# Side tasks of the first feed forward layer with fp32 products in place of split ones

## The chip, the cores and the metric

The kernel runs on one core of one Trainium2 chip. The metric is the device time of one execution in microseconds: three runs of the kernel before gave 1909.66, 1913.12 and 1913.76 us, median 1913.12 us. The profiled execution was a fourth one.

## The reference

Two blocks run one after the other on a sequence of 256 positions of width 1024, all in fp32. The first block has two layers; each is a mixer (three kinds of attention) and a feed forward layer. The second block also has two layers: the first mixes by long convolutions (Hyena), the second by attention; both have a cross attention on a memory and sixteen experts. Cut to what the change touches:

```python
# first block, layer l
x = x + hybrid_mixer(rms_norm(x, norm_mix[l]), ...)
x = x + jnp.square(jax.nn.relu(rms_norm(x, norm_mlp[l]) @ w_up[l])) @ w_down[l]     # 1024 -> 4096 -> 1024

# second block: needs nothing of x
h = jnp.sin(fr * (feats @ w1 + b1))                       # 256 x 33 -> 256 x 64
h = jnp.sin(fr * (h @ w2 + b2))                           # 256 x 64
h = (h @ w3).reshape(L, 2, 2, 768) * decay                # the filter layer: order, direction, channel
h = h / (jnp.sum(jnp.abs(h), axis=(0, 2), keepdims=True) + 1e-6)
k_fft = jnp.fft.rfft(two_sided(h), axis=0)                # the spectra
mem_n = rms_norm_2(mem, mem_norm_g)
mk, mv = jnp.split(mem_n @ w_mem_kv[i], 2, axis=-1)       # the memory projections, i = 0, 1; 256 + 256 columns
```

## The kernel before, in words

A product of two fp32 matrices is mostly done as three fp32r products (`mm3`, L302): each operand is split into a rounded part (hi, xh) and a rest (lo, xl), and hi·hi, lo·hi and hi·lo are summed in PSUM. The rounding is a copy on ScalarE (L290); the rest is a subtraction (L291) that GpSimd and VectorE take in turn. A product written with plain fp32 operands needs no split; the trace shows it as two TensorE instructions.

The first feed forward layer (`mlp`, about 246 to 540 us of the trace) is a sequence of units. A unit has a `prep` (load and split a weight tile) and a `run` (its products); `Pipe` prepares two units ahead of the one that it runs. Weight tiles of 1 MB come through a ring of five buffers over the queue of SyncE, in program order: a load waits until its buffer is free. A buffer becomes free with the last instruction that reads it. Up products go to `psT`, down products to `acc`.

What the second block needs of constants and memory is computed beside this layer, in a generator (`mlp0_tasks`). After each unit `Pipe.tick` lets it take one step, up to its next `yield`, and so the instructions of a step stand, on every engine's in-order queue, between those of two units. `filters_task` first loads small tables and makes the two sine layers (`sin_layer`, on VectorE and ScalarE), with `h2` as their result on 128 partitions: the 64 hidden rows stand there twice. Then it goes through four blocks (order o, half n of the channels). A block has two steps of the filter layer (`psf`, L1119 and L1120, one for each 128 positions, two directions d in each), their sums and differences over the directions (`hx`, then split into `hs`), the column sums of the absolute values (`sab`, `psn`, `nrm`), and two steps of spectra (L303 to L305 into `psf`, then `ke` and `kx`). `memory_task` normalises and transposes the memory (`Norm`, two halves of 512 columns) and computes, for both layers, keys (`psT`) and values (`psM`). `Norm` transposes on TensorE into PSUM (L343); ScalarE copies the rounded part out (L346), and VectorE the rest (L347). A PSUM buffer is free once both have read it. Four PSUM buffers (`A`) serve `psT`, `psf`, `psn`, `psM` and the transposes of the memory in turn.

The order on each engine is fixed when the program is built. Before the last down products the layer waits for the side tasks to end (`pipe.join(side)`), and all later stages follow it.

Of the kernel before, what the change touches and what calls it, by code (L numbers as in the profile page):

```python
# [22 lines left out]
T = 256  # L23
# [176 lines left out]
def build(ctx, tc, I, C, out, upto="all", dbg=None):  # L200
# [124 lines left out]
    class Norm:  # L325
# [3 lines left out]
        def __init__(self, src, g, pool=None, psum=None, split=True):  # L329
            self.src, self.g, self.ps = src, g, psum or B  # L330
            if split:
                self.xh = (pool or xtp).tile([128, 8, T], F32R, tag="xh", name="xh")
                self.xl = (pool or xtp).tile([128, 8, T], F32R, tag="xl", name="xl")
            self.ss = small.tile([128, 2, 2], F32, tag="ss", name="ss")
            self.halves = 0
            self.r = self.R = None

        def half(self, n):
            for k2 in (4 * n, 4 * n + 2):
# [690 lines left out]
    def stream(units, pool):  # L1030

        ahead = deque()
        for u in units + [None, None]:
            if u:
                hl.append(pool)
                u.prep()
                hl.pop()
                ahead.append(u)
            if len(ahead) == 3 or not u:
                ahead.popleft().run()  # L1040
            yield

# [17 lines left out]
    def filters_task(ring, kd):  # L1060

        with tc.tile_pool(name="fl", bufs=1) as fp:
# [26 lines left out]
            hst = fp.tile([128, T], F32R, name="fhst")  # L1089
# [3 lines left out]
            S.activation(hst, h2, AF.Copy)  # L1093
            V.tensor_tensor(hst[64:], h2[64:], hst[64:].bitcast(F32), op=ALU.subtract)
# [5 lines left out]
            for o in range(2):  # L1100
                for n in range(2):
                    c = slice(384 * n, 384 * n + 384)
                    w3 = fp.tile([128, 2, 384], F32, name="fw3")
                    for d in range(2):
                        nc.sync.dma_start(w3[64 * d:64 * d + 64], I["hy_filt_w3_2"][0].rearrange("k (o d c) -> k o d c", o=2, d=2)[:, o, :, c])
                    w3h = fp.tile([128, 2, 384], F32R, name="fw3h")
                    w3l = fp.tile([64, 2, 384], F32R, name="fw3l")
                    S.activation(w3h, w3, AF.Copy)
                    G.tensor_tensor(w3l, w3[:64], w3h[:64].bitcast(F32), op=ALU.subtract)
                    hs = {op: [fp.tile([128, 2, 384], F32R, tag=f"h{op}{i}", name="hs") for i in range(2)] for op in (ALU.add, ALU.subtract)}  # L1110
                    sab = fp.tile([128, 384], F32, tag="sab", name="sab")
                    yield
                    for t in range(2):
                        hd = []
                        for d in range(2):
# [26 lines left out]
                    for part, op in ((0, ALU.add), (1, ALU.subtract)):  # L1142
# [3 lines left out]
                        for t in range(2):  # L1146
                            mm3(pp[t], Fh[:, t, part], Fl[:, t, part], hs[op][0][:, t], hs[op][1][:, t], True, True)
# [10 lines left out]
    def memory_task(ring, mp, sp, m, kvd):  # L1158

        nm = Norm(m, gain("mem_norm_g_2"), mp, A)  # L1160
        yield from nm.task(lambda n: True)
        for l in range(2):
# [3 lines left out]

            def put_k(j, ps):
                V.tensor_tensor(kv[:, 0], ps, nm.R[:, None, :].to_broadcast([128, 2, T]), op=ALU.mult)

            def put_v(ps):  # L1170
                for t in range(2):
                    evac(kv[:, 1, t], ps[t][:, :256], t, nm.r[:, t:t + 1])
# [658 lines left out]
    def mlp0_tasks(ring):  # L1831
        yield from filters_task(ring, kd)
        with tc.tile_pool(name="memp", bufs=1) as mp, tc.tile_pool(name="mems", bufs=3) as sp:
# [4 lines left out]
            yield from memory_task(ring, mp, sp, m, kvd)  # L1838
# [183 lines left out]
```

## Time and profile before

| | us |
|---|---|
| three runs: lowest, median, highest | 1909.66, 1913.12, 1913.76 |
| the profiled execution's own time | 1915.09 |
| its span, first to last instruction | 1913.3 |
| TensorE busy | 1643.7 (86%) |
| VectorE busy | 981.1 (51%) |
| ScalarE busy | 665.7 (35%) |
| GpSimd busy | 540.2 (28%) |
| mean granted TensorE clock | 0.952 |

Busy time is an average over stages with different limits: in the page's 40 slices of 47.8 us TensorE is busy nine tenths through most of the first half, and from slice 24 on the DMA engines are. In a row of the trace PE is a product on TensorE and PEld its weight load; DVE is VectorE, ACT ScalarE, POOL GpSimd, SPq the queue of SyncE. A form such as `64*128 64x384` means weights on 64 rows and 128 columns, and 384 columns streamed. A product's duration includes the time until its end has come out, so consecutive products overlap; the pace is read from their starts. A bracket at a row's end holds the idle time of the engine before it, and whose result ended it.

### The profile page before, as it was taken

The numbers are of one execution on the slowest core, as the hardware profiler recorded it, in microseconds if no ns is written. First come the engines' busy times: TensorE is split into PE (matmuls) and PEld (weight loads), VectorE is DVE, ScalarE is ACT, GpSimd is POOL, SyncE is SP. The second block draws the span as 40 slices with busy tenths as digits, with TensorE's granted clock in tenths as the row PEclk, the third lists the DMA queues.
The fourth block names the chain that finished last, engine by engine and source line by source line (L and its number), as shares of the span: only waits on it lengthen the run. The fifth ranks groups of instructions, "written<-read, shape, count | busy, mean of one in ns | idle before, by whom it ended". The sixth has DMA issues, their size and how long they took to land. (4 is left out here: it accounts for less than half of the span.)

```text
span 1913.3 us, 27291 instructions
## 1 busy us (share of the span) xinstructions
PE 1643.7 (86%) x11139; PEld 1201.3 (63%) x11139; DVE 981.1 (51%) x1642; ACT 665.7 (35%) x1100; POOL 540.2 (28%) x330
## 2 busy tenths in 40 slices
PE   8899988999998999999989989676667999766665
PEld 7898977788988979899978765222224655211221
DVE  7987467666489865754568763010104873100102
ACT  4346444454443464545444432000003552000000
POOL 4532455754445325444434220000002220000001
PEclk9999999999999999999999989898988999898987
DMA  6443554455633435755443679999999768999997
GB/s 237 128 133 123 179 181 157 162 194 170 211 125 102 161 124 174 259 196 182 152 160 121 221 285 420 425 425 425 425 413 335 265 247 362 425 426 424 426 420 254
DMA packets 136516, 490.42 MB, mean 256 GB/s; under 512 B 11152, under 2 KB 32067, under 8 KB 115911
## 3 DMA queue, kind: packets, MB, share of 16 engines
q1 hardware_dynamic: 135919, 488.11, 67.8%
q8 instruction: 87, 1.43, 0.3%
q10 hardware_dynamic: 472, 0.57, 0.1%
q14 instruction: 38, 0.31, 0.0%
HBM read 483.41 MB, written 5.24 MB: 255 GB/s over the span
## 5 line engine op out<-in xcount | busy, mean ns | idle before, releaser
L291 POOL TENSOR_TENSOR lo<-w,hi 128x1024 fp32r<-128x1024 f32 (+3 forms) x163 | 379.1, 2327 | 806.5 <-ACT hi L290 776.4
L290 ACT ACTIVATE hi<-w 128x1024 fp32r<-128x1024 f32 (+3 forms) x330 | 327.3, 997 | 347.7 <-PE psT L305 178.9
L304 PE MATMUL psT<-xh,lo 128*128 128x256 f32 x1328 | 382.1, 288 | 12.4 <-POOL lo L291 12.4
L303 PE MATMUL psT<-xh,hi 128*128 128x256 f32 x1328 | 388.6, 293 | 2.0 <-ACT hi L290 2.0
L305 PE MATMUL psT<-xl,hi 128*128 128x256 f32 x1328 | 381.6, 287 | 0.0
L291 DVE TENSOR_TENSOR lo<-w,hi 128x1024 fp32r<-128x1024 f32 (+3 forms) x167 | 223.2, 1337 | 145.4 <-ACT hi L290 144.7
L304 PEld LDWEIGHTS psT<-xh,lo 128*128 128x128 f32 x1328 | 259.5, 195 | 18.1 <-POOL lo L291 14.2
L303 PEld LDWEIGHTS psT<-xh,hi 128*128 128x128 f32 x1328 | 259.2, 195 | 10.1 <-issue 5.9
L305 PEld LDWEIGHTS psT<-xl,hi 128*128 128x128 f32 x1328 | 259.3, 195 | 1.8 <-issue 1.8
L1738 PE MATMUL psx<-w,late 128*32 128x256 f32 (+1 forms) x1024 | 155.3, 539 | 75.8 <-DMA w<-in_exp_w_up 40.5
L1738 PEld LDWEIGHTS psx<-w,late 128*32 128x32 f32 x1024 | 47.0, 115 | 181.5 <-issue 74.2
L1738 PE MATMUL psx<-w,xg 128*32 128x256 f32 (+1 forms) x1024 | 124.1, 538 | 36.6 <-DMA w<-in_exp_w_up 19.9
L1790 PE MATMUL psy<-w,late 128*32 128x512 f32 x576 | 95.3, 596 | 38.2 <-DMA w<-in_exp_w_down 34.3
L1774 ACT ACTIVATE yy<-psy,rslot 128x512 fp32r<-128x512 f32 (+1 forms) x17 | 11.3, 662 | 320.7 <-PE psy L1790 249.7
L1738 PEld LDWEIGHTS psx<-w,xg 128*32 128x32 f32 x1024 | 39.9, 116 | 117.5 <-issue 60.6
L305 PE MATMUL acc<-lo,hh 128*128 128x512 f32 x256 | 100.7, 393 | 1.9 <-POOL lo L291 1.9
L304 PE MATMUL acc<-hi,hlo 128*128 128x512 f32 x256 | 100.8, 394 | 0.0
L303 PE MATMUL acc<-hi,hh 128*128 128x512 f32 x256 | 100.5, 393 | 0.0
L1982 POOL TENSOR_TENSOR o<-X,gf 128x256 f32<-128x256 f32 (+1 forms) x6 | 6.1, 1042 | 326.5 <-DVE X L1780 326.5
L1775 DVE SCALAR_TENSOR_TENSOR yy<-psy,rslot,yy 128x512 fp32r<-128x512 f32 (+1 forms) x17 | 12.2, 719 | 163.4 <-ACT yy L1774 162.9
L1754 DVE TENSOR_TENSOR late<-late,psx 128x512 f32<-128x512 f32 (+1 forms) x16 | 8.1, 550 | 166.8 <-PE psx L1738 166.8
L1790 PEld LDWEIGHTS psy<-w,late 128*32 128x32 f32 x576 | 26.6, 109 | 102.6 <-DMA w<-in_exp_w_down 52.4
(494 smaller groups left out, 2945.3 us busy)
## 6 DMA issues: line engine op xcount, KB each, us to landing
w<-in_exp_w_gate SPq DMA_DIRECT2D x64, 1536.0 KB, 27.8
w<-in_exp_w_up SPq DMA_DIRECT2D x64, 1536.0 KB, 29.5
w<-in_exp_w_down SPq DMA_DIRECT2D x48, 1536.0 KB, 28.5
w<-in_w_in SPq DMA_DIRECT2D x39, 1024.0 KB, 5.1
w<-in_w_up SPq DMA_DIRECT2D x32, 1024.0 KB, 5.7
w<-in_w_down SPq DMA_DIRECT2D x32, 1024.0 KB, 6.8
w<-in_exp_w_down SPq DMA_DIRECT2D x18, 1024.0 KB, 14.3
w<-in_w_out SPq DMA_DIRECT2D x10, 1024.0 KB, 5.6
```

What stands on the lines that cost most here:

```text
L290: S.activation(hi, src, AF.Copy)
L291: next(lo_engines[0]).tensor_tensor(lo, src, hi.bitcast(F32), op=ALU.subtract)
L303: PE.matmul(ps, lh, rh, start=start, stop=False)
L304: PE.matmul(ps, ll, rh, start=False, stop=False)
L305: PE.matmul(ps, lh, rl, start=False, stop=stop)
L1738: mm = PE.matmul(pg[nm][n][32 * e:32 * e + 32, :c1 - c0], xg[gr // 2][:, k, 128 * (gr % 2) + 32 * e:128 * (gr % 2) + 32 * e + 32], wt[e][: ...
L1754: V.tensor_tensor(hid[:, c], sg[:, :n], pg["up"][i][:, :n], op=ALU.mult)
L1774: S.activation(yh, py, AF.Copy, scale=rs[:, 2, gr:gr + 1])
L1775: V.scalar_tensor_tensor(yl, py, rs[:, 2, gr:gr + 1], yh.bitcast(F32), op0=ALU.mult, op1=ALU.subtract)
L1790: PE.matmul(py[n][32 * e:32 * e + 32], hT[:, k, 32 * e:32 * e + 32], wt[e][:, k - k0, 512 * n:512 * n + 512], start=k == 0, stop=k == 5, t ...
L1982: G.tensor_tensor(o[:, t, c], X[:, t, c], gf[:, c], op=ALU.mult)
```

## The change

Three places of the side tasks lose their splits:

- Filter layer: the sum over 64 hidden rows was one product over 128 rows (both parts of `h2` against the rounded weights) and one over 64 rows (against the weights' rest), for each direction. Now each direction is one fp32 product over 64 rows; direction 0 uses partitions 0 to 63 and direction 1 partitions 64 to 127 (`tile_position`), and each has its own PSUM buffer. The weights `w3` come in half the size, in two buffers. The conversions of `h2` (`hst`) and `w3` (`w3h`, `w3l`) go.
- Spectra: the constant transform `F` and the sums `hs` stay fp32, and three fp32r products become one fp32 product. `F` is loaded alone; before, it took a ring buffer and was split into `Fh` and `Fl`.
- Memory projections: `Norm` gets a third form (`split=None`) that writes one fp32 tile by ScalarE alone. Keys and values are fp32 products straight from the ring's weight tiles, in 8 steps per layer where there were 11. `stream` goes.

```diff
         def __init__(self, src, g, pool=None, psum=None, split=True):
-            if split:
+            self.x = None
+            if split is None:
+                self.x = pool.tile([128, 8, T], F32, name="xT")
+            elif split:
...
                 for j in range(2):
                     k = k2 + j
+                    if self.x is not None:
+                        S.activation(self.x[:, k], ps[:, j], AF.Copy, scale=self.g[:, k:k + 1])
+                        continue
...
-            raw = ring.one(C["fwd"]).rearrange("p t (s f) -> p t s f", s=2)[:, :, :, :128]
-            Fh = fp.tile([128, 2, 2, 128], F32R, name="fFh")
-            Fl = fp.tile([128, 2, 2, 128], F32R, name="fFl")
-            S.activation(Fh, raw, AF.Copy)
-            V.tensor_tensor(Fl, raw, Fh.bitcast(F32), op=ALU.subtract)
+            F = fp.tile([128, 2, 2, 128], F32, name="fF")
+            nc.sync.dma_start(F, C["fwd"].rearrange("p t (s f) -> p t s f", s=2)[:, :, :, :128])
...
-            S.activation(hst, h2, AF.Copy)
-            V.tensor_tensor(hst[64:], h2[64:], hst[64:].bitcast(F32), op=ALU.subtract)
...
-                    w3 = fp.tile([128, 2, 384], F32, name="fw3")
+                    w3 = fp.tile([128, 384], F32, name="fw3", bufs=2)
...
-                    S.activation(w3h, w3, AF.Copy)
-                    G.tensor_tensor(w3l, w3[:64], w3h[:64].bitcast(F32), op=ALU.subtract)
...
+                        pd = [A("psf", [128, 384]) for _ in range(2)]
+                        for d in range(2):
+                            r = slice(64 * d, 64 * d + 64)
+                            PE.matmul(pd[d], h2[r, sl], w3[r], start=True, stop=True, tile_position=(64 * d, 0))
                         for d in range(2):
                             h = fp.tile([128, 384], F32, tag=f"hd{d}", name="hd")
-                            ps = A("psf", [128, 384])
-                            sl = slice(t * 128, (t + 1) * 128)
-                            PE.matmul(ps, hst[:, sl], w3h[:, d], start=True, stop=False)
-                            PE.matmul(ps, hst[:64, sl], w3l[:, d], start=False, stop=True)
-                            V.tensor_tensor(h, ps, dec[:, t, c], op=ALU.mult)
+                            V.tensor_tensor(h, pd[d], dec[:, t, c], op=ALU.mult)
...
-                            x = fp.tile([128, 384], F32, tag="hx", name="hx")
-                            V.tensor_tensor(x, hd[0], hd[1], op=op)
-                            S.activation(dst[0][:, t], x, AF.Copy)
-                            G.tensor_tensor(dst[1][:, t], x, dst[0][:, t].bitcast(F32), op=ALU.subtract)
+                            V.tensor_tensor(dst[:, t], hd[0], hd[1], op=op)
...
-                            mm3(pp[t], Fh[:, t, part], Fl[:, t, part], hs[op][0][:, t], hs[op][1][:, t], True, True)
+                            PE.matmul(pp[t], F[:, t, part], hs[op][:, t], start=True, stop=True)
...
-        nm = Norm(m, gain("mem_norm_g_2"), mp, A)
+        nm = Norm(m, gain("mem_norm_g_2"), mp, A, None)
...
-            yield from stream(dense_T(ring, None, nm.xh, nm.xl, put_k, tiles=[x[:, :, :256] for x in w]), sp)
-            yield from stream(dense_M(ring, None, nm.xh, nm.xl, put_v, tiles=[x[:, :, 256:] for x in w]), sp)
+            yield
+            ps = A("psT", [128, 2, T])
+            for i in range(2):
+                for q in range(2):
+                    for k in range(4):
+                        PE.matmul(ps[:, q], w[i][:, k, 128 * q:128 * q + 128], nm.x[:, 4 * i + k],
+                                  start=i == 0 and q == 0 and k == 0, stop=i == 1 and q == 1 and k == 3)
+                yield
+            V.tensor_tensor(kv[:, 0], ps, nm.R[:, None, :].to_broadcast([128, 2, T]), op=ALU.mult)
+            ps = [A("psM") for _ in range(2)]
+            for k0 in range(0, 8, 2):
+                for t in range(2):
+                    for k in (k0, k0 + 1):
+                        PE.matmul(ps[t][:, :256], nm.x[:, k, t * 128:(t + 1) * 128], w[k // 4][:, k % 4, 256:],
+                                  start=k == 0, stop=k == 7)
+                yield
+            for t in range(2):
+                evac(kv[:, 1, t], ps[t][:, :256], t, nm.r[:, t:t + 1])
```

On TensorE, a step of the filter layer stood like this before (`psT` is an up product of the feed forward layer, `psf` the step; each L1119 and L1120 is one instruction):

```order
L305 MATMUL psT<-xl,hi 128x256
L1119 MATMUL psf<-fw3h,fhst 128x384
L1120 MATMUL psf<-fw3l,fhst 128x384
L1119 MATMUL psf<-fw3h,fhst 128x384
L1120 MATMUL psf<-fw3l,fhst 128x384
L303 MATMUL psT<-xh,hi 128x256
```

and so after the change:

```order
L303 MATMUL psT<-xh,hi 128x256
L304 MATMUL psT<-xh,lo 128x256
L305 MATMUL psT<-xl,hi 128x256
L1102 MATMUL psf<-fw_3173,fh_3085 128x384 x2
L303 MATMUL psT<-xh,hi 128x256
```

Four products, alternately over 128 and 64 rows, became two fp32 products over 64 rows each, between the same two units.

On VectorE, where the output projection of the mixer before ends (`X` is the residual sum of one half of the positions, `xl` the rest of the normalised transposes, `lo` a weight split), the rows before are

```order
L291 TENSOR_TENSOR lo<-w,hi 128x1024
L465 TENSOR_TENSOR X<-psM,X 128x512
L1079 TENSOR_TENSOR fFl<-w,fFh 128x512
L465 TENSOR_TENSOR X<-psM,X 128x512
L354 SCALAR_TENSOR_TENSOR junk,ss<-X 128x512
L347 SCALAR_TENSOR_TENSOR xl<-pst,cols,xh 128x256 x4
```

and after the change

```order
L949 TENSOR_TENSOR ml<-gate,mh 128x512
L291 TENSOR_TENSOR lo<-w,hi 128x1024
L471 TENSOR_TENSOR X<-psM,X 128x512 x2
L360 SCALAR_TENSOR_TENSOR junk,ss<-X 128x512
L353 SCALAR_TENSOR_TENSOR xl<-pst,cols,xh 128x256 x4
```

The subtraction for the constant transform stood between the two residual sums and is gone; they now follow each other.

On ScalarE, at the transposes of the memory (`xh` before, `xT` now; `hi` a weight split, the one of 512 columns for the memory's values), the rows before are

```order
L353 ACTIVATE junk,ss<-mem 128x512
L290 ACTIVATE hi<-w 128x1024 x4
L290 ACTIVATE hi<-w 128x512
L290 ACTIVATE hi<-w 128x1024 x2
L346 ACTIVATE xh<-pst,cols 128x256 x4
```

and after the change

```order
L359 ACTIVATE junk,ss<-mem 128x512
L290 ACTIVATE hi<-w 128x1024 x4
L350 ACTIVATE xT<-pst,cols 128x256 x4
L290 ACTIVATE hi<-w 128x1024
L350 ACTIVATE xT<-pst,cols 128x256 x4
```

The splits of the memory's weights no longer stand ahead of the copies, and the VectorE rows that read the same PSUM buffers (`xl` of the memory) have no counterpart.

## Rows read from the trace of the kernel before

**Rows 1.** Busy time by engine in four stretches; times in us, instruction counts in brackets.

```profile
core 0: us, PE busy (x) PEld busy (x) DVE busy (x) ACT busy (x) POOL busy (x), PEclk, DMA share, GB/s
246.00:300.00 54.00, 44.28 (x240) 35.98 (x238) 39.09 (x61) 26.71 (x39) 23.94 (x12) 0.94 0.53 170
300.00:420.00 120.00, 113.24 (x659) 95.76 (x659) 82.95 (x85) 60.69 (x90) 76.07 (x46) 0.99 0.48 162
455.00:535.00 80.00, 80.00 (x539) 73.22 (x538) 39.63 (x41) 36.20 (x49) 38.11 (x19) 1.00 0.56 192
880.00:970.00 90.00, 90.00 (x554) 80.98 (x553) 46.08 (x34) 44.13 (x53) 39.34 (x17) 1.00 0.43 145
```

**Rows 2.** The chain of waits at its entry into the expert layers: start, us, what.

```profile
1152.50 2.83 PE psx L1738 x32
1155.34 15.84 DMA w<-in_exp_w_down
```

**Rows 3.** TensorE in order of time, first layer: start, us, line, tiles, idle before and releaser.

```profile
260.55 0.44 PE L343 MATMUL pst<-ident,X 128*128 128x128 f32 x2 [1.39 <-DVE X L465]
...
263.46 1.54 PE L343 MATMUL pst<-ident,X 128*128 128x128 f32 x6 [1.54 <-DVE X L465]
...
299.29 0.44 PE L1119 MATMUL psf<-fw3h,fhst 128*128 128x384 f32 x1 [4.06 <-DVE fhst L1094]
...
450.25 1.03 PE L343 MATMUL pst<-ident,mem 128*128 128x128 f32 x4 [3.55 <-DVE xl L347]
```

**Rows 4.** Waits of TensorE from 300 to 460: total us, times, longest.

```profile
PE psf L303 <- DVE nrm L1140: 3.6, 4, 0.9
...
PE acc L305 <- POOL lo L291: 1.9, 3, 0.8
PE psn L1139 <- POOL sab L1127: 1.2, 2, 0.6
```

**Rows 5.** VectorE in order of time, same columns, at the places of rows 3 and 4.

```profile
260.42 2.39 DVE L1079 TENSOR_TENSOR fFl<-w,fFh 128x512 fp32r<-128x512 f32 x1
262.73 0.68 DVE L465 TENSOR_TENSOR X<-psM,X 128x512 f32<-128x512 f32 x1
...
294.35 2.45 DVE L1057 TENSOR_SCALAR sa<-sa 128x256 f32<-128x256 f32 x1
...
317.36 2.73 DVE L1132 TENSOR_TENSOR hx<-hd 128x384 f32<-128x384 f32 x1 [3.69 <-POOL hs L1134]
...
449.62 0.88 DVE L347 SCALAR_TENSOR_TENSOR xl<-pst,cols,xh 128x256 fp32r<-128x256 f32 x2
```

**Rows 6.** Busy time by engine in three stretches at a reduced TensorE clock.

```profile
262.60:269.40 6.80, 5.94 (x17) 4.96 (x18) 4.00 (x9) 2.87 (x5) 0.00 (x0) 0.50 0.88 325
...
300.10:303.50 3.40, 3.40 (x14) 2.74 (x13) 2.05 (x4) 1.05 (x2) 1.00 (x1) 0.51 0.85 271
...
450.30:453.70 3.40, 3.40 (x17) 3.40 (x18) 2.79 (x6) 2.32 (x5) 0.00 (x0) 0.50 0.16 33
```

**Rows 7.** TensorE in order of time: 256-column products, fp32r first, then fp32.

```profile
428.05 0.28 PE L303 MATMUL psT<-xh,hi 128*128 128x256 f32 x1
...
430.03 0.28 PE L305 MATMUL psT<-xl,hi 128*128 128x256 f32 x1
...
115.79 1.03 PE L721 MATMUL psi<-ikbd,iqT 128*128 128x256 f32 x4
...
118.74 0.59 PE L721 MATMUL psi<-ikbd,iqT 128*128 128x256 f32 x2
```

**Rows 8.** TensorE in order of time, one step of the filter layer.

```profile
329.99 0.34 PE L1119 MATMUL psf<-fw3h,fhst 128*128 128x384 f32 x1
330.26 0.44 PE L1120 MATMUL psf<-fw3l,fhst 64*128 64x384 f32 x1
...
331.36 0.38 PE L303 MATMUL psT<-xh,hi 128*128 128x256 f32 x1
```

**Rows 9.** TensorE in order of time, four fp32 products on 32-column tiles.

```profile
1154.67 0.61 PE L1738 MATMUL psx<-w,xg 128*32 128x256 f32 x8
```

More of the change, by code (lines that the diff above doesn't have):

```diff
@@ L1028, in wait @@
             yield
[L1030 to L1041, printed above, removed]
     def sin_layer(ps, b, fr, out, pool):
@@ L1088, in filters_task @@
             h2 = fp.tile([128, T], F32, name="fh2")
-            hst = fp.tile([128, T], F32R, name="fhst")
             ps = A("psf", [128, T])
@@ L1102, in filters_task @@
                     c = slice(384 * n, 384 * n + 384)
-                    w3 = fp.tile([128, 2, 384], F32, name="fw3")
+                    w3 = fp.tile([128, 384], F32, name="fw3", bufs=2)
                     for d in range(2):
-                        nc.sync.dma_start(w3[64 * d:64 * d + 64], I["hy_filt_w3_2"][0].rearrange("k (o d c) -> k o d c", o=2, d=2)[:, o, :, c])
-                    w3h = fp.tile([128, 2, 384], F32R, name="fw3h")
-                    w3l = fp.tile([64, 2, 384], F32R, name="fw3l")
-                    S.activation(w3h, w3, AF.Copy)
-                    G.tensor_tensor(w3l, w3[:64], w3h[:64].bitcast(F32), op=ALU.subtract)
-                    hs = {op: [fp.tile([128, 2, 384], F32R, tag=f"h{op}{i}", name="hs") for i in range(2)] for op in (ALU.add, ALU.subtract)}
+                        nc.sync.dma_start(w3[64 * d:64 * d + 64], I["hy_filt_w3_2"][0].rearrange("k (o d c) -> k o d c", o=2, d=2)[:, o, d, c])
+                    hs = {op: fp.tile([128, 2, 384], F32, tag=f"h{op}", name="hs") for op in (ALU.add, ALU.subtract)}
                     sab = fp.tile([128, 384], F32, tag="sab", name="sab")
@@ L1114, in filters_task @@
                         hd = []
+                        sl = slice(t * 128, (t + 1) * 128)
+                        pd = [A("psf", [128, 384]) for _ in range(2)]
+                        for d in range(2):
+                            r = slice(64 * d, 64 * d + 64)
+                            PE.matmul(pd[d], h2[r, sl], w3[r], start=True, stop=True, tile_position=(64 * d, 0))
                         for d in range(2):
                             h = fp.tile([128, 384], F32, tag=f"hd{d}", name="hd")
-                            ps = A("psf", [128, 384])
-                            sl = slice(t * 128, (t + 1) * 128)
-                            PE.matmul(ps, hst[:, sl], w3h[:, d], start=True, stop=False)
-                            PE.matmul(ps, hst[:64, sl], w3l[:, d], start=False, stop=True)
-                            V.tensor_tensor(h, ps, dec[:, t, c], op=ALU.mult)
+                            V.tensor_tensor(h, pd[d], dec[:, t, c], op=ALU.mult)
                             if t == 0 and d == 0:
@@ L1156, in filters_task, with memory_task @@
             V.reciprocal(rn, nrm)
-    def memory_task(ring, mp, sp, m, kvd):
-        nm = Norm(m, gain("mem_norm_g_2"), mp, A)
+    def memory_task(ring, mp, m, kvd):
+        nm = Norm(m, gain("mem_norm_g_2"), mp, A, None)
         yield from nm.task(lambda n: True)
@@ L1165, in memory_task @@
             yield
-            def put_k(j, ps):
-                V.tensor_tensor(kv[:, 0], ps, nm.R[:, None, :].to_broadcast([128, 2, T]), op=ALU.mult)
-            def put_v(ps):
-                for t in range(2):
-                    evac(kv[:, 1, t], ps[t][:, :256], t, nm.r[:, t:t + 1])
-            yield from stream(dense_T(ring, None, nm.xh, nm.xl, put_k, tiles=[x[:, :, :256] for x in w]), sp)
-            yield from stream(dense_M(ring, None, nm.xh, nm.xl, put_v, tiles=[x[:, :, 256:] for x in w]), sp)
+            yield
[9 more added lines that the diff above has]
+            for k0 in range(0, 8, 2):
+                for t in range(2):
+                    for k in (k0, k0 + 1):
[4 more added lines that the diff above has]
+                evac(kv[:, 1, t], ps[t][:, :256], t, nm.r[:, t:t + 1])
             nc.sync.dma_start(kvd[l], kv)
@@ L1832, in mlp0_tasks @@
         yield from filters_task(ring, kd)
-        with tc.tile_pool(name="memp", bufs=1) as mp, tc.tile_pool(name="mems", bufs=3) as sp:
+        with tc.tile_pool(name="memp", bufs=1) as mp:
             m = mp.tile([128, 2, D], F32, name="mem")
@@ L1837, in mlp0_tasks @@
                 yield
-            yield from memory_task(ring, mp, sp, m, kvd)
+            yield from memory_task(ring, mp, m, kvd)
     c2s = ctx
```

## Prediction

> **What bounds the kernel now.** I read the busy time by stretches first. Where the feed forward layer runs without filter or transpose steps beside it, TensorE is busy without a gap: 80.00 of 80 us, and 90.00 of 90 us in the same layer of the second pass. Where those side tasks run it is busy 44.28 of 54 and 113.24 of 120 us, with no other engine above 82.95 of 120 [rows 1]. So TensorE's in-order queue sets the pace there, and the side tasks put idle time into it. Next, the chain: it enters the expert layers over a product of TensorE at 1152.50 and is the weight transfers' from 1155.34 on [rows 2]. All that stands before follows the feed forward layer in order, and I take it that a microsecond gained there is one at the end. Then TensorE's rows with idle time ahead of them [rows 3], the sums of its waits [rows 4], what VectorE did in those moments [rows 5], and the clock [rows 6]. ScalarE and GpSimd lose work too; I cost that at nothing by itself, since they are busy 60.69 and 76.07 of 120 us, and count only what TensorE waits for.
>
> **Added and removed on TensorE.** Pace first. From 428.05 to 430.03 stand 18 fp32r products of 256 columns: 1.98 / 17 = 0.117 us each, so 0.35 for the three of one split product. Four fp32 instructions of 256 columns take 1.03 us and two take 0.59: 0.22 each, and a product has two, 0.44 [rows 7]. For 384 columns I scale by 1.5: 0.525 and 0.66 us, which no row shows at that size.
> - Memory projections: per layer 16 products for keys and 16 for values, 64 in all, by 0.09 more: +5.8 us.
> - Spectra: four blocks, two parts, two positions, 16 products by 0.135 more: +2.2 us.
> - Filter layer: a step took 331.36 - 329.99 = 1.37 us, though four instructions of 384 columns at pace are 0.70. The rest goes with the crossings between 128-row and 64-row weights: 330.26 - 329.99 is 0.27 us, 0.10 over the pace, on the way in [rows 8], which leaves 0.57 for the other three, 0.19 each. The new step has one crossing in and one out, 0.29. If its two products run side by side it is 0.66 + 0.29 = 0.95 us, if one after the other 1.32 + 0.29 = 1.61. For 8 steps that is -3.4 or +1.9 us. No row shows two row groups at once. The nearest shows four column groups: eight fp32 instructions of 256 columns in 0.61 us, hardly more than the 0.59 of two on full columns [rows 9, 7]. I take side by side, -3.4, and keep +1.9 for the range.
>
> Sum on TensorE: 5.8 + 2.2 - 3.4 = +4.6 us, or +9.9.
>
> The Trainium skill ("TensorE: Matmul & The Clock Gate", Part 3, packing) says that tiles of different row groups overlap and start about 4 ns apart; by that the step would be the 0.95 us. No run so far shows it for rows, so the sum stands on the column groups.
>
> **Waits removed.**
> - At 263.46 TensorE waits 1.54 us for the second residual sum X [rows 3]. VectorE made that at 262.73, behind the 2.39 us of the transform's subtraction fFl [rows 5], which goes. I take 1.5; what is late next is the split weight for the product behind.
> - At 299.29 it waits 4.06 us for fhst, the converted h2 [rows 3]. The conversion on two engines goes, and the chain ahead of it gets earlier, because the first w3 conversion leaves ScalarE and GpSimd. The clamp at 294.35, 2.45 us long beside a GpSimd split [rows 5], may then come before that split. Bounds: 0.8 us (two short conversions alone) and 4.06. I take 3.0.
> - In the four blocks TensorE waits 3.6 us for nrm, 1.9 for the rests of down weights from GpSimd, 1.2 for sab [rows 4], 6.7 in all. The first comes of VectorE's queue, where nrm stands behind the difference hx, which waits 3.69 us for GpSimd's split of hs and then takes 2.73 [rows 5]; the other two of GpSimd itself, which loses the splits of hs and w3. I take 6.0, with 3.0 and 6.7 as bounds.
> - At 450.25 the second half of the memory's transposes waits 3.55 us for xl [rows 3], which VectorE ends with two subtractions at 449.62 [rows 5], behind splits that GpSimd stretches. The rest goes, and ScalarE's copy alone frees the buffer, with 24 up products as cover. I take 3.5.
>
> Sum: 14.0 us, with 7 and 16 as bounds.
>
> **Clock.** Right behind three of these waits the granted clock is 0.50, 1.2 in place of 2.4 GHz: 6.80 us from 262.60, 3.40 us from 300.10 and from 450.30 [rows 6]. At half speed that costs 3.4 + 1.7 + 1.7 = 6.8 us. The first has another idle time ahead of it that stays (1.39 us at 260.55 [rows 3]). I take the third whole, most of the second and a part of the first: 4.5, bounds 0 and 6.8.
>
> **Costed at nothing.** Fewer side steps only end the side task earlier inside the layer. The memory's weights now occupy two ring buffers until TensorE has used them, where the splits freed them; between the release and the products that use the load behind it stand, by the order, at least 96 up products, 96 x 0.117 = 11 us, as cover, and if that failed, TensorE would wait for the load by as much as it is late. The weights w3 have two buffers, so that SyncE's queue doesn't stop for them.
>
> **Sum.** 14.0 + 4.5 - 4.6 = 13.9 us less than the profiled execution's 1915.1, so 1901.2. That execution lies 2.0 above the median of the three runs, 1913.1; against the median it is 1899.
>
> **Rivals.**
> - *The pair doesn't overlap*: +9.9 in place of +4.6, so 8.6 less, 1904.5. For it: no row shows row groups at once. Against: [rows 9].
> - *All waits and all lost clock go*: 16 + 6.8 - 4.6 = 18.2 less, 1895; with the shorter waits that no group lists, down to 1892.
> - *VectorE is still held up*: its long rows stand beside GpSimd's splits of the layer's own weights, and these stay. The sums hs are now written at the place of hx and can be stretched just so; then nrm stays late, fhst's successor comes a little earlier, and only 7 of the waits and 2 of the clock go: 7 + 2 - 4.6 = 4.4 less, 1908.7. For it: the clamp of 2.45 us had no split of the side tasks beside it. Against: what held hx was GpSimd's split of hs, which is gone. The Trainium skill ("SBUF — State Buffer", on the two separate sides) says that VectorE and GpSimd lock a shared pair of ports for a whole instruction, and that the loser waits; that is this case, and the lengths of [rows 5] agree.
> - *The waits are given back* (slower): the place is the first unit behind each side step. Its weights' rests come from the same two engines, so TensorE, no longer late, would wait there instead. Then nothing goes but +4.6 comes, 1917.7 against the median, 1923 if the pair doesn't overlap either. It decides from the point at which less than 4.6 us of the 18.5 in waits and clock stays gained. For it: 1.9 us of waits for just these rests [rows 4]. Against: with the same splits and no side steps there is no gap in 80 and 90 us [rows 1].
>
> **How the numbers follow.** Chances: the forecast 0.47; the pair not overlapping 0.15; all gone 0.12; VectorE still held up 0.16; given back 0.10. The terms' bounds (7 to 16 of waits, 0 to 6.8 of clock) give 1895 to 1911 against the median; "all gone" and the scatter of the three runs, 4.1 us, take the lower end to 1890, and 1911 takes in "still held up". What stays out is "given back" and the tails, about two in ten. A change below 0.2%, 3.8 us, can't be told from none here. Faster by more than that (below 1909.3): the first three cases and half of the fourth, 0.82. Within it: 0.10. Slower: 0.08.
>
> **What would show it.** A filter step of about 0.95 us on TensorE, the second product's first instruction starting with the first's; a memory product of 0.44 us; no idle time ahead of the transposes of X and of the memory; no nrm or sab among TensorE's waits; the clock at full speed around 300 and 450 us; TensorE busy over 0.97 between 300 and 420 us. I am wrong if the side steps' waits come back at the following units, or if the layer ends earlier and the end does not.

## The result, and the profile after

The changed kernel took 1891.09 us, median of 6 runs (1887.42 to 1896.56), beside 1912.95 us of the kernel before (6 runs, 1909.66 to 1913.76). The ratio is 0.989, with a 95% interval of 0.9873 to 0.9907: faster by 21.9 us, where 14 were forecast. The profiled execution took 1891.49 us, its span 1889.6, its mean granted clock 0.959; that is 23.6 us less than the profiled one before.

Four stretches of the layer after the change, same columns as [rows 1]: PE, PEld, DVE, ACT and POOL busy, then the granted clock.

```profile
246.00:300.00 54.00, 50.72 (x314) 42.40 (x313) 42.91 (x67) 28.97 (x43) 23.92 (x12) 1.00 0.58 186
300.00:405.00 105.00, 104.29 (x625) 87.28 (x624) 67.03 (x80) 51.00 (x69) 50.79 (x27) 1.00 0.54 184
405.00:440.00 35.00, 35.00 (x225) 31.68 (x224) 23.35 (x32) 18.82 (x29) 15.50 (x6) 1.00 0.61 208
440.00:515.00 75.00, 72.85 (x402) 63.65 (x400) 31.19 (x46) 24.56 (x35) 20.14 (x11) 1.00 0.54 183
```

TensorE lacks 0.71 of 105 us where the filter and the spectra run; before it lacked 6.8 of 120 [rows 1]. The 2.15 us that it lacks in the last stretch are its wait for the next norm at the layer's end, which both kernels have (2.50 and 2.45 us, below). The clock is 1.00 in all four; the three stretches at 0.50 [rows 6] have no counterpart. Next, TensorE's rows that answer to [rows 3] (start, us, line, tiles, idle before and releaser):

```profile
259.07 0.44 PE L346 MATMUL pst<-ident,X 128*128 128x128 f32 x2 [1.37 <-DVE X L471]
259.81 0.82 PE L346 MATMUL pst<-ident,X 128*128 128x128 f32 x6
...
280.11 0.70 PE L1080 MATMUL psf<-fh,fw 64*128 64x256 f32 x2 [0.29 <-ACT fh L1051]
287.67 0.99 PE L1102 MATMUL psf<-fw,fh 64*128 64x384 f32 x4
...
422.78 1.03 PE L346 MATMUL pst<-ident,mem 128*128 128x128 f32 x8
```

The wait at 260.55 stays (1.37 us). The second transposes of X, the first filter step and the second half of the memory's transposes, now one row of eight, have no bracket. Of the sums of waits in [rows 4] one is left, TensorE's waits from 300 to 405 us:

```profile
PE psf L1128 <- DVE nrm L1121: 0.7, 1, 0.7
```

The ledger is made of starts that exist in both traces: the second sine layer's product, the first down product `acc`, one behind the fourth block, the row sums `psr` behind the memory's transposes, a down product behind the last projections, and `psr` of the next norm, where the layer ends. First the kernel before, then the changed one:

```profile
287.11 0.70 PE L1091 MATMUL psf<-fh,fw 64*128 64x256 f32 x2 [1.14 <-ACT fh L1058]
311.54 0.40 PE L303 MATMUL acc<-hi,hh 128*128 128x512 f32 x1
416.15 0.39 PE L303 MATMUL acc<-hi,hh 128*128 128x512 f32 x1
455.10 0.60 PE L370 MATMUL psr<-ident,nrb 128*128 128x128 f32 x4
517.73 0.40 PE L303 MATMUL acc<-hi,hh 128*128 128x512 f32 x1
539.39 1.23 PE L370 MATMUL psr<-ident,nrb 128*128 128x128 f32 x4 [2.50 <-DVE nrb L365]
```

```profile
298.13 0.40 PE L303 MATMUL acc<-hi,hh 128*128 128x512 f32 x1
393.62 0.69 PE L303 MATMUL acc<-hi,hh 128*128 128x512 f32 x1
426.46 0.60 PE L376 MATMUL psr<-ident,nrb 128*128 128x128 f32 x4
493.51 0.58 PE L303 MATMUL acc<-hi,hh 128*128 128x512 f32 x1
515.30 0.72 PE L376 MATMUL psr<-ident,nrb 128*128 128x128 f32 x4 [2.45 <-DVE nrb L371]
```

Before the stage that changed, at 243 us, the changed kernel's execution was already 1.5 us early. The pieces, as gains (the last column divides the forecast's 4.5 us of clock as 1.2, 1.6 and 1.7, which it had left in words):

| piece | before | after | gain, us | forecast |
|---|---|---|---|---|
| to the second sine layer's product (from 1.5 early) | 287.11 | 280.11 | 5.5 | 1.5 + 1.2 |
| to the first down product | 311.54 | 298.13 | 6.4 | 3.0 + 1.6 + 0.4 |
| to the end of the four blocks | 416.15 | 393.62 | 9.1 | 6.0 + 3.0 - 2.2 |
| memory's transposes | 455.10 | 426.46 | 6.1 | 3.5 + 1.7 |
| memory's projections | 517.73 | 493.51 | -4.4 | -5.8 |

Together 22.7 us against 13.9. At the layer's end the lead is 24.1 us and at the end of the program 23.7, so in this pair of traces nothing of it is given back later.

### The profile page after: what moved, and what is told of

Its sections match the earlier page's. It is cut to its first block, busy times and chain, and to the rows that moved or that the text cites. A ratio compares the mean times of both kernels' runs of the same rounds, so it can differ in the third digit from the quotient of the medians.

```text
span 1889.6 us, 27034 instructions
## 1 busy us (share of the span) xinstructions
PE 1633.1 (86%) x11059; PEld 1191.0 (63%) x11059; DVE 951.2 (50%) x1626; ACT 647.0 (34%) x1066; POOL 502.7 (27%) x304
## 5 line engine op out<-in xcount | busy, mean ns | idle before, releaser
L291 POOL TENSOR_TENSOR lo<-w,hi 128x1024 fp32r<-128x1024 f32 (+3 forms) x157 | 367.9, 2344 | 831.3 <-ACT hi L290 792.4
L290 ACT ACTIVATE hi<-w 128x1024 fp32r<-128x1024 f32 (+3 forms) x318 | 318.9, 1006 | 380.6 <-PE psT L305 175.0
L304 PE MATMUL psT<-xh,lo 128*128 128x256 f32 x1296 | 370.8, 286 | 12.6 <-POOL lo L291 11.7
L303 PE MATMUL psT<-xh,hi 128*128 128x256 f32 x1296 | 378.0, 292 | 2.2 <-ACT hi L290 2.2
L305 PE MATMUL psT<-xl,hi 128*128 128x256 f32 x1296 | 370.3, 286 | 0.0
L291 DVE TENSOR_TENSOR lo<-w,hi 128x1024 fp32r<-128x1024 f32 (+3 forms) x161 | 212.1, 1317 | 156.5 <-ACT hi L290 152.1
L304 PEld LDWEIGHTS psT<-xh,lo 128*128 128x128 f32 x1296 | 250.9, 194 | 17.9 <-POOL lo L291 13.2
L303 PEld LDWEIGHTS psT<-xh,hi 128*128 128x128 f32 x1296 | 251.0, 194 | 12.9 <-issue 8.2
L305 PEld LDWEIGHTS psT<-xl,hi 128*128 128x128 f32 x1296 | 250.9, 194 | 1.5 <-issue 1.5
L303 PE MATMUL acc<-hi,hh 128*128 128x512 f32 x256 | 104.5, 408 | 0.0
```

What stands on the lines that cost most here:

```text
L290: S.activation(hi, src, AF.Copy)
L291: next(lo_engines[0]).tensor_tensor(lo, src, hi.bitcast(F32), op=ALU.subtract)
L303: PE.matmul(ps, lh, rh, start=start, stop=False)
L304: PE.matmul(ps, ll, rh, start=False, stop=False)
L305: PE.matmul(ps, lh, rl, start=False, stop=stop)
```

## The experiments

Ratios are against the kernel before, differences in us against the changed kernel unless another is named. Experiments 1 to 4 ran beside the kernel before at 1913.41 us (7 runs); 5, 6, 7 and the first half of 10 at 1914.89 (15 runs); 8, 9 and the second half of 10 at 1912.09 (7 runs).

The medians of several of these kernels lie within their scatter, and much of the scatter comes from behind the layer: from the start of `psr` of the next norm to the end of the program the thirteen traces take 1367.1 to 1374.3 us. No run here tells what decides on that. The layer itself, from the first transpose of X to that `psr`, can be compared more closely, by trace, in us:

| kernel | layer |
|---|---|
| before | 278.8 |
| changed; once more (experiment 9) | 256.2; 259.1 |
| memory undone (1) | 257.7 |
| spectra undone (2) | 268.7 |
| filter layer undone (3) | 266.8 |
| pair in series (4) | 262.9 |
| second reader (5) | 258.8 |
| kernel before, conversion moved (6) | 277.9 |
| conversion of the transform back (7) | 260.4 |
| split of the sums back (8) | 267.1 |
| both halves of the memory part (10), twice | 253.5; 253.7 |

The changed kernel's second trace has a wait of 1.7 us that its first lacks (experiment 9). The traces of experiments 2, 4, 5, 7 and 8 have it too, and are best compared with the 259.1; that of experiment 3 lacks it. Experiment 3 also shows the scatter at its worst: its layer is 10.5 us longer than 256.2, its median only 6.6 us higher, and its trace has the shortest part behind the layer (1367.1).

**1. Memory part undone.** Split projections and the two-reader `Norm` are back.

```diff
-        nm = Norm(m, gain("mem_norm_g_2"), mp, A, None)
+        nm = Norm(m, gain("mem_norm_g_2"), mp, A)
...
+            yield from stream(dense_T(ring, None, nm.xh, nm.xl, put_k, tiles=[x[:, :, :256] for x in w]), sp)
```

> The changed kernel with the memory part undone: normalised memory and its projections split again, filter layer and spectra as changed. Theory (waits and clock): the wait ahead of the second half of the memory's transposes comes back (3.6 us) and the half clock behind it (1.7), and the products are 4.4 us shorter again: about 1891.1 + 5.3 - 4.4 = 1892. Rival (only the work on TensorE counts): 1891.1 - 4.4 = 1886.7.

Measured: 1889.16 us (1888.53 to 1893.97, 4 runs), ratio 0.988 (0.9851 to 0.9909). By runs it can't be told from the changed kernel. In the trace the wait for xl is back, and behind it 3.41 us at half clock:

```profile
428.27 1.00 PE L346 MATMUL pst<-ident,mem 128*128 128x128 f32 x4 [3.55 <-DVE xl L353]
```

At `psr` behind the memory's transposes this trace is 6.7 us later than the first of the changed kernel, 0.6 of it from ahead of the transposes of X, and the shorter products give 4.4 back. So the memory part is two effects of opposite sign, close to nothing in sum: the fp32 products by themselves are a loss.

**2. Spectra undone.** `F` and `hs` are split again, with three fp32r products.

```diff
-            F = fp.tile([128, 2, 2, 128], F32, name="fF")
+            S.activation(Fh, raw, AF.Copy)
+            V.tensor_tensor(Fl, raw, Fh.bitcast(F32), op=ALU.subtract)
...
+                            G.tensor_tensor(dst[1][:, t], x, dst[0][:, t].bitcast(F32), op=ALU.subtract)
```

> The changed kernel with the spectra undone: F and hs split again, three fp32r products each. Theory (waits and clock): the subtraction fFl again stands between the two residual sums (1.5 us of wait, up to 3.4 of clock), the waits for nrm come back (3.6 us), the products are 2 us shorter: 1894 to 1898. Rival (only the work on TensorE counts): 1889.

Measured: 1900.61 us (1899.39 to 1902.56, 4 runs), ratio 0.9933 (0.991 to 0.9955), more than the 1894 to 1898 of the theory. First the second transposes of X and the stretch right behind them, then TensorE's waits from 300 to 425 us:

```profile
262.65 0.87 PE L346 MATMUL pst<-ident,X 128*128 128x128 f32 x6 [1.54 <-DVE X L471]
```

```profile
262.60:269.40 6.80, 6.75 (x33) 5.69 (x34) 3.67 (x7) 3.72 (x6) 0.52 (x1) 1.00 0.96 370
```

```profile
PE psf L303 <- DVE nrm L1127: 5.6, 4, 1.4
PE acc L305 <- POOL lo L291: 1.7, 3, 0.8
PE acc L305 <- DVE lo L291: 0.6, 1, 0.6
```

The wait for X is as long as before (1.54 us [rows 3]), yet the clock stays at 1.00. The splits of the spectra alone bring 7.9 us of waits into the blocks.

**3. Filter layer undone.** The converted `hst`, `w3h` and `w3l` are back.

```diff
-                            PE.matmul(pd[d], h2[r, sl], w3[r], start=True, stop=True, tile_position=(64 * d, 0))
...
+                            PE.matmul(ps, hst[:, sl], w3h[:, d], start=True, stop=False)
+                            PE.matmul(ps, hst[:64, sl], w3l[:, d], start=False, stop=True)
```

> The changed kernel with the filter layer undone: h2 and w3 converted again, four products over 128 and 64 rows in turn. Theory (waits and clock): a step takes 1.37 us again in place of about 0.94 (3.4 us over 8 steps), the wait for fhst comes back (2 to 4 us) and the half clock behind it (0 to 1.7): 1897 to 1900. Rival (only the work on TensorE counts): 1894.5.

Measured: 1897.71 us (1895.58 to 1902.08, 4 runs), ratio 0.9919 (0.9894 to 0.9945). The wait for fhst is back in full, and the clock behind it is 0.50 for 6.8 us, which costs 3.4 us where 1.7 at most were expected:

```profile
293.89 0.44 PE L1109 MATMUL psf<-fw3h,fhst 128*128 128x384 f32 x1 [4.00 <-DVE fhst L1084]
```

```profile
294.30:301.10 6.80, 6.80 (x27) 5.81 (x27) 3.03 (x6) 1.79 (x4) 1.29 (x1) 0.50 0.64 239
```

This holds although spectra and memory are as after the change, so the filter layer's own conversions cost the 4 us; this edit puts back those of `h2` and of `w3` together. The trace tells two parts apart. One is the clamp at the end of the second sine layer, which is the first row here (VectorE, then GpSimd), and the second fence has it in the changed kernel:

```profile
288.95 2.44 DVE L1050 TENSOR_SCALAR sa<-sa 128x256 f32<-128x256 f32 x1
288.79 2.45 POOL L291 TENSOR_TENSOR lo<-w,hi 128x1024 fp32r<-128x1024 f32 x1 [3.72 <-ACT hi L290]
```

```profile
286.88 0.29 DVE L1050 TENSOR_SCALAR sa<-sa 128x256 f32<-128x256 f32 x1
288.64 2.41 POOL L291 TENSOR_TENSOR lo<-w,hi 128x1024 fp32r<-128x1024 f32 x1 [5.15 <-ACT hi L290]
```

The chain ahead is 1.6 us later here (the second sine layer's product starts at 281.69, in the changed kernel at 280.11; 0.6 of it comes from ahead of the layer), and so the clamp, which in the changed kernel comes 1.8 us ahead of GpSimd's split, stands beside it and takes 2.15 us longer. The other part is the conversion of `h2`: `h2` is ready at 291.85 and its converted form at 293.83, 2.0 us later. Each is about half of the wait.

**4. The pair in series.** Both directions use rows 0 to 63.

```diff
-                            PE.matmul(pd[d], h2[r, sl], w3[r], start=True, stop=True, tile_position=(64 * d, 0))
+                            PE.matmul(pd[d], h2[:64, sl], w3[:, d], start=True, stop=True)
```

> The changed kernel with both directions' products on rows 0 to 63, so that they can't run side by side; nothing else changes. Theory (TensorE's queue is the path at these steps): each of the 8 steps is longer by one product's two instructions, 0.65 us, 5.2 in all: 1896.3. Rival (the steps have slack, or the pair doesn't gain by standing side by side): 1891.

Measured: 1893.03 us (1890.81 to 1895.98, 4 runs), ratio 0.9893 (0.9869 to 0.9917): runs don't tell it from the changed kernel. The trace does. One filter step and the next product, first of the changed kernel, then in series:

```profile
316.44 0.92 PE L1102 MATMUL psf<-fw,fh 64*128 64x384 f32 x4
317.29 0.39 PE L303 MATMUL psT<-xh,hi 128*128 128x256 f32 x1
```

```profile
317.07 1.55 PE L1101 MATMUL psf<-fw,fh 64*128 64x384 f32 x4
318.56 0.38 PE L303 MATMUL psT<-xh,hi 128*128 128x256 f32 x1
```

A step is 0.85 us and 1.48 in series (the starts have more digits in the trace: 0.845 and 1.484), 0.64 more in each of eight steps, 5.1 us. Behind the blocks this trace is 6.9 us later, 1.7 of it by a wait that experiment 9 explains; the wait of 0.7 us for nrm, which the changed kernel kept, is gone here, so a part of the longer steps is hidden.

**5. A second reader put back.** VectorE reads the memory's transposes from PSUM again; nothing uses what it writes.

```diff
+                        V.scalar_tensor_tensor(self.xl[:, k], ps[:, j], self.g[:, k:k + 1], self.x[:, k], op0=ALU.mult, op1=ALU.subtract)
```

> The changed kernel with one thing put back: VectorE reads each of the memory's transposes from PSUM again and subtracts (the result is used by nothing). Theory (the 3.6 us came of VectorE's queue, where other splits stood ahead of these reads, and of GpSimd's split stretching them): with the queue relieved, the wait at the second half is below 1 us and the clock stays at 1.00; about 1892 us. Rival (a second reader of the buffer is the wait in itself): 3.6 us of wait and 1.7 us of lost clock come back, about 1896 us.

Measured: 1892.53 us (1889.19 to 1893.52, 4 runs), ratio 0.9886 (0.9867 to 0.9906). The transposes don't wait, and VectorE itself waits for ScalarE (second fence):

```profile
426.74 1.03 PE L347 MATMUL pst<-ident,mem 128*128 128x128 f32 x8
430.42 1.03 PE L347 MATMUL pst<-ident,mem 128*128 128x128 f32 x8
```

```profile
428.16 0.88 DVE L352 SCALAR_TENSOR_TENSOR xl<-pst,cols,xT 128x256 fp32r<-128x256 f32 x2 [0.53 <-ACT xT L351]
```

The rival falls: a second reader by itself makes no wait here. The 3.55 us of [rows 3] took what stood ahead of that reader on VectorE as well. Before the change those were rests of weights and, among others, two operations on 128x2 elements, each over two microseconds long while GpSimd was at two splits (VectorE, then GpSimd, kernel before):

```profile
440.92 2.34 DVE L321 TENSOR_TENSOR rt<-rt,nr 128x2 f32<-128x2 f32 x1
...
443.79 2.35 DVE L322 SCALAR_TENSOR_TENSOR nr<-rt,nr 128x2 f32<-128x2 f32 x1
446.17 0.16 DVE L320 TENSOR_TENSOR rt<-rh,nr 128x2 f32<-128x2 f32 x1
```

```profile
440.05 6.06 POOL L291 TENSOR_TENSOR lo<-w,hi 128x1024 fp32r<-128x1024 f32 x2 [4.25 <-ACT hi L290]
```

Either half can be taken away: experiment 10 keeps the memory's weight splits on VectorE and drops the second reader, and its transposes wait 0.64 us at most.

**6. The transform's conversion moved, in the kernel before.**

```diff
-            S.activation(Fh, raw, AF.Copy)
-            V.tensor_tensor(Fl, raw, Fh.bitcast(F32), op=ALU.subtract)
...
             G.memset(ones, 1.0)
+            S.activation(Fh, raw, AF.Copy)
+            V.tensor_tensor(Fl, raw, Fh.bitcast(F32), op=ALU.subtract)
```

> The kernel before with one thing changed: the conversion of the transform (Fh, Fl) stands behind the second sine layer, no longer between the two residual sums. Theory (the low clock behind the second residual sum hangs on this wait of 1.5 us): the wait goes and with it 3.4 us of lost clock, some 5 us less, 1908 us. Rival (the clock does not hang on this wait alone): 1.5 us less at most, 1911.5 us or above, with the clock at 0.50 still in a stretch behind the transposes of X.

Measured: 1913.85 us (1911.84 to 1921.18, 10 runs), ratio 0.9998 (0.9986 to 1.0011). The experiment missed its aim: on VectorE the subtraction still stands between the two residual sums (first fence; they start at 258.87 and 261.79), so the wait is not removed. It shows something else, the same wait with the clock at 1.00 behind it:

```profile
259.47 2.40 DVE L1096 TENSOR_TENSOR fFl<-w,fFh 128x512 fp32r<-128x512 f32 x1
```

```profile
262.53 0.87 PE L343 MATMUL pst<-ident,X 128*128 128x128 f32 x6 [1.56 <-DVE X L465]
```

```profile
262.60:269.40 6.80, 6.80 (x33) 5.71 (x34) 3.66 (x7) 3.72 (x6) 0.64 (x1) 1.00 0.98 370
```

**7. The transform's conversion put back**, unused, with its load, in the changed kernel.

```diff
+            raw = ring.one(C["fwd"]).rearrange("p t (s f) -> p t s f", s=2)[:, :, :, :128]
...
+            S.activation(Fh, raw, AF.Copy)
+            V.tensor_tensor(Fl, raw, Fh.bitcast(F32), op=ALU.subtract)
```

> The changed kernel with the conversion of the transform put back at its old place between the two residual sums (its results are used by nothing, and its load through the ring comes back). Theory: the wait of 1.5 us at the second transposes comes back and the low clock behind it too, 1.5 + 3.4 us more, about 1896 us. Rival: the wait alone comes back, at the full clock as in the kernel with the spectra undone, about 1893 us.

Measured: 1896.02 us (1895.3 to 1897.29, 4 runs), ratio 0.9908 (0.989 to 0.9927). The wait comes back (1.56 us), with the clock at 1.00:

```profile
264.16 0.88 PE L346 MATMUL pst<-ident,X 128*128 128x128 f32 x6 [1.56 <-DVE X L471]
```

```profile
264.20:271.00 6.80, 6.80 (x33) 5.75 (x34) 3.69 (x7) 3.72 (x6) 0.63 (x1) 1.00 0.99 351
```

So the subtraction fFl is what held the second residual sum. It takes 2.40 us here, beside a split of GpSimd that starts 0.53 us ahead of it, and 2.39 in [rows 5]; the rest of a weight tile of the same size and types took VectorE 0.68 us (at 443.19, kernel before). So nearly all of the wait is what that meeting adds. The median is 3.5 us above that of experiment 5, where the trace accounts for the wait alone; whether the low clock came in other executions, which have no profile here, stays open.

**8. The split of the sums put back**, in its form, with the products left as they are.

```diff
-                            V.tensor_tensor(dst[:, t], hd[0], hd[1], op=op)
+                            x = fp.tile([128, 384], F32, tag="hx", name="hx")
+                            V.tensor_tensor(x, hd[0], hd[1], op=op)
+                            S.activation(dst[:, t], x, AF.Copy)
+                            G.tensor_tensor(rest[op][:, t], x, dst[:, t], op=ALU.subtract)
```

> The changed kernel with the split of the sums hs put back in its form: VectorE writes hx, ScalarE copies it to hs, GpSimd subtracts the two (a rest that nothing uses); the products stay single fp32 ones. Theory (the waits of the four blocks come of hx standing behind GpSimd's subtraction): four waits of 0.9 us or more for nrm and some for the rests of down weights come back, 5 to 8 us in all, with the low clock nowhere: 1896 to 1899 us. Rival (they came of the conversions of w3 and the longer filter step before, which stay away here): TensorE waits less than 2 us more in the blocks, about 1892 us.

Measured: 1899.93 us (1894.6 to 1902.07, 4 runs), beside 1891.34 of the changed kernel in experiment 9, and just over the 1896 to 1899 of the theory; ratio 0.9927 (0.9905 to 0.9949). Waits from 300 to 410 us:

```profile
DVE hx L1117 <- POOL rest L1119: 15.4, 7, 2.2
PE psf L1132 <- DVE nrm L1125: 5.1, 4, 1.3
PE acc L305 <- POOL lo L291: 0.9, 2, 0.6
PE acc L305 <- DVE lo L291: 0.6, 1, 0.6
```

The chain of the forecast stands here in one view: VectorE waits 15.4 us for GpSimd before hx, and TensorE behind it 5.1 for nrm and 1.5 for weights; the clock stays at 1.00. The 8.6 us between the medians, and the 8.0 us by which the layer is longer in the traces, are more than the 6.6 us of TensorE's waits in this list; the rest has no owner. The rival falls, since the conversions of w3 are away.

**9. The changed kernel once more.**

> The changed kernel itself once more, beside the two others of this call: 1889 to 1893 us if its time does not depend on the day's runs.

Measured: 1891.34 us (1888.73 to 1892.25, 4 runs), ratio 0.9884 (0.9867 to 0.9901). Its trace has a wait that the first trace of the very same program lacks, and its cause on VectorE and GpSimd (second fence):

```profile
419.97 0.51 PE L305 MATMUL acc<-lo,hh 128*128 128x512 f32 x1 [1.72 <-DVE lo L291]
```

```profile
416.31 2.23 DVE L365 TENSOR_TENSOR ms<-ss 128x2 f32<-128x2 f32 x1
...
418.69 1.22 DVE L291 TENSOR_TENSOR lo<-w,hi 128x1024 fp32r<-128x1024 f32 x1
415.79 2.73 POOL L291 TENSOR_TENSOR lo<-w,hi 128x1024 fp32r<-128x1024 f32 x1 [0.67 <-ACT hi L290]
```

It is the first trace that is the exception. Eight traces here are of kernels with the fp32 memory part, and six of them have this wait, 1.72 to 1.74 us long, behind an operation `ms` of 2.2 us (experiments 2, 4, 5, 7, 8 and 9); the first trace of the changed kernel and experiment 3 don't. The three with split memory products behind the new filter layer (experiments 1 and 10, twice) don't either.

**10. Both halves of the memory part that pay.** One fp32 copy of the transposes by ScalarE, split from SBUF by ScalarE and GpSimd, and split products.

```diff
+        for i in range(2):
+            c = slice(4 * i, 4 * i + 4)
+            S.activation(nm.xh[:, c], nm.x[:, c], AF.Copy)
+            G.tensor_tensor(nm.xl[:, c], nm.x[:, c], nm.xh[:, c].bitcast(F32), op=ALU.subtract)
+            yield
...
+            yield from stream(dense_T(ring, None, nm.xh, nm.xl, put_k, tiles=[x[:, :, :256] for x in w]), sp)
```

> The changed kernel with the memory projections split again (three fp32r products), while the transposes keep their one fp32 copy by ScalarE; the split of that copy is made from SBUF, by ScalarE and GpSimd. Theory (the wait at the memory's transposes came of the PSUM buffer's second reader, and the fp32 products cost 4.4 us): no wait of 3.6 us and no low clock at the transposes, products shorter by 4.4 us, so about 1887 us. Rival (the split queue is the wait, wherever it is read from): a wait of 2 us or more for xl or for the split weights comes at the first memory products, and the time is 1890 or above.

Measured: 1887.68 us (1886.69 to 1889.72, 5 runs), ratio 0.9864 (0.9845 to 0.9883). It ran again, beside experiment 9:

> The kernel with split memory projections behind a single fp32 copy once more, beside the changed kernel. Theory (its trace lost 1.5 of the 4.4 us to two short waits and kept 2.7): 2 to 4 us below the changed kernel of this call. Rival (what is gained on TensorE's queue is lost to chance waits elsewhere): no difference that the runs can tell, within 1.5 us.

Measured: 1886.38 us (1885.4 to 1888.55, 4 runs), ratio 0.9864 (0.9844 to 0.9884), against 1891.34: 5.0 us below, and its slowest run lies below the fastest of the other. TensorE's waits of this second trace:

```profile
424.30 0.66 PE L346 MATMUL pst<-ident,mem 128*128 128x128 f32 x4 [0.64 <-ACT xT L350]
435.30 0.50 PE L305 MATMUL acc<-lo,hh 128*128 128x512 f32 x1 [0.74 <-POOL lo L291]
```

Two short waits take 1.4 of the 4.4 us, and the layer's end stands at 513.06, where the changed kernel has 515.30. A part of the 5 us is the wait of experiment 9, which neither trace of this kernel has: its layer is about 2.7 us shorter than the changed kernel's without that wait, and about 5.5 us shorter than with it. The two ratios' intervals overlap, so the 5 us rest on this one comparison and on the traces.

## Why the prediction was right, and where its sizes were off

The time lies in the range, the direction and the mechanism are those forecast; the gain was 22 us where 14 were forecast. The second rival, "all waits and all lost clock go" (1892 to 1895), came nearest; the median is 0.9 us past its end. Step by step:

- *TensorE bounds the layer, and what is gained there is one gain at the end*: held. 24.1 us at the layer's end became 23.7 at the program's. That the two agree so closely is luck: for the changed kernel's second trace they are 20.7 and 23.1, since the part behind the layer takes 1371.6 us there and 1374.3 in the first.
- *The pair runs side by side*: held, at 0.85 us for a forecast 0.95. Against 1.37 [rows 8] that is 8 x 0.52 = 4.2 us in place of 3.4. Experiment 4 shows that in series the steps take 5.1 us more, which was the first rival's price of 5.3; the layer is only 3.8 us longer in its trace than in the changed kernel's with the same wait, as other waits get shorter.
- *Spectra*: a pair of fp32 products (337.18 to 338.70, less the 0.23 of one down product) takes 1.29 us where six fp32r instructions at pace take 1.05: +1.9 for a forecast +2.2. *Memory*: +4.4 for +5.8. The whole term was +2.1 and not +4.6, and this is the first mis-sized term: 2.5 us.
- *X, 1.5 us*: held. Experiment 7 brings it back with the conversion alone.
- *fhst*: taken at 3.0 for bounds of 0.8 and 4.06; all of it went, and 0.85 us ahead of it at fh (1.14 to 0.29 us of idle time), which no group listed. Experiment 3 brings it back at 4.00 with spectra and memory changed. That the clamp would come before GpSimd's split, which the prediction thought possible, is what happened (0.29 us in place of 2.44), and so the upper bound was the value to take. The lower bound was too low: the conversions, with what stands ahead of them in their queues, take 2.0 us and not 0.8.
- *The four blocks*: 6.0 forecast from 6.7 listed; one wait of 0.7 us is left. Experiment 8 shows the chain as written. "VectorE is still held up" did not come about (one wait of 0.7 us), and the same run says why: it needs GpSimd's split of the sums, not those of the layer's weights.
- *xl, 3.5 us*: held in size, and 0.8 us went with it that no group listed (TensorE at 443.30, waiting for a weight's rest from GpSimd). The reason takes two things: the reader on VectorE, and a long queue ahead of it there. Experiment 5 shortens the queue and experiment 10 takes away the reader, and neither has the wait. What GpSimd stretched were the two operations on 128x2 elements, to 2.34 and 2.35 us; the weights' rests on VectorE, which the prediction took to be stretched, took 0.7 and 1.2 us.
- *Clock, 4.5 us*: 6.8 went between these two traces, the second mis-sized term. But 3.4 of it, behind X, does not go with the wait alone: the same wait stands in experiments 2, 6 and 7 with the clock at 1.00, in 6 with the kernel before nearly unchanged. That the profiled execution of the kernel before had the low clock there is chance as far as these traces tell. Behind fhst and xl it fell in every trace that has the wait of 3.5 us or more (the kernel before, and experiments 1, 3 and 6). Taking only a part of the first stretch was the right reading. The medians differ by 21.9 us where the traces differ by 23.6.
- *Given back*: in the first trace nothing was, but that is luck too. The rests of weights, which were to become late instead, have no wait there; in six of the eight traces with the fp32 memory part one of them makes TensorE wait 1.7 us behind the blocks (experiment 9). So this rival came about in small, and the ledger's 6.1 us for the memory's transposes is the better of two cases.

The terms as measured (waits of 1.5, 4.1, 0.85, 6.0, 3.55 and 0.8, clock 6.8, less 2.1 of work) come to 21.5 of the ledger's 22.7 us; the rest has no owner.

What stays open is what decides on the clock behind a wait of 1.5 us; it is one trace against three. Behind the wait for the next norm at the layer's end, 2.4 to 2.5 us in all thirteen traces, it is ten against three: the granted clock of the next 3.4 us is 0.52 to 0.59 in ten, and 1.00 in experiments 2 and 5 and the second trace of 10.

## What to carry to other kernels

Cost a split not by its own instructions but by who stands behind it: here the splits of three small side tasks cost some 25 us of waits and lost clock on TensorE (22.7 gained and 2.1 paid), and products slower by 2 us in all removed them. Then ask whether the slower product is needed at all: in the memory part the reader that came late had to go, not the split, and a kernel that keeps the memory's split products and splits from another place was 3 to 5 us faster still. Where the runs of two kernels overlap, a start that both traces share tells more than their medians; but take more than one trace, since the same program had two times in this layer.

## What the runs showed of the hardware

Two fp32 products on different row groups run side by side, instruction by instruction. The first two of the step at 316.44 (the four of it are shown in experiment 4):

```profile
316.44 0.59 PE L1102 MATMUL psf<-fw,fh 64*128 64x384 f32 x2
```

They start 6 ns apart and each takes 0.587 us by itself, so both are over within 0.59 us. In series the four take 1.48 us to the next product, side by side 0.85.

An operation of VectorE on 256 numbers takes 0.16 us, and took 2.2 to 2.4 us where it met a split of 128x1024 on GpSimd (experiments 5 and 9). Which one of a row of small operations is hit depends on less than a microsecond: in the first trace of the changed kernel, where `ms` starts 0.41 us ahead of the split, it was one behind the weight's rest that TensorE needed; in the second, where `ms` starts 0.52 us behind the split's start, it was `ms`, ahead of that rest. So one program has two times in this layer, 2.7 us apart behind this place. The Trainium skill ("SBUF — State Buffer", "SBUF: two separate sides") says that VectorE and GpSimd lock a shared pair of ports for a whole instruction and that the loser blocks; the 2.23 us beside 0.16 agree: that operation ends 0.02 us after the split beside it.
